# Moving the tiles of a hybrid DeltaNet / gMLP layer to other byte offsets, and folding an identity product into the inverse's residual

## The chip, the core and the metric

The kernel runs on one core of a Trainium2 chip. A core has five engines that run their own instruction streams and meet through semaphores: PE (TensorE, matrix products), DVE (VectorE), ACT (ScalarE), POOL (GpSimd) and SP (SyncE, which here issues every DMA). PE has a second row in the profile, PEld, for the loading of the stationary operand. Operands lie in SBUF, a memory of 128 partitions; a tile takes the same byte range of every partition, and "address" below means the byte within a partition. Products are summed in PSUM. The metric is the device time of one execution in microseconds (us); of several runs the median is given.

## What is computed

One layer of a diffusion backbone over 17 tiles of 128 tokens (one tile of context, sixteen of latent tokens), model width 1024:

```
h = rmsnorm(x, norm_mix) * (1 + sc1) + sh1
o = mixer(h)                      # [gated DeltaNet, both directions | gMLP] -> w_out
x = x + ga1 * o
h = rmsnorm(x, norm_ffn) * (1 + sc2) + sh2
x = x + ga2 * (square(relu(h @ w_ff1)) @ w_ff2)        # 1024 -> 4096 -> 1024
y = rmsnorm(x, norm_final)
```

In the DeltaNet every chunk needs a triangular solve:

```
a_mat = where(strict, (k_beta @ k.T) * decay, 0)
sol = triangular_solve(a_mat + I, rhs, lower=True, unit_diagonal=True)
```

## The kernel before

**Products in two pieces.** Nearly all large products are float32 products made of three float32r products: an operand is split into a rounded part H and the rest L, and `mm3` (L222 to L228) issues, for each stationary pair and moving pair, H·H (L226), H·L (L227) and L·H (L228). Each is one matmul with a stationary operand of 128x128 and a moving operand of up to 512 columns.

**Stages, in the order of the program.** First the modulation, the norms and the projections to q, k, v (blocks of 3 tiles, moving operands of 386, 388 or 258 columns, tiles `kH` and `kL`). Then the scan: 34 units (17 tiles, two directions), each with a prepared inverse and a chain of states, between which "fillers" run (the projections to gate, u, v of the gMLP, its spatial product with `wsT`, the output projection and the second norm). Then the MLP: 32 units of the first product (FF1), each 7 products (a Strassen-like scheme over halves of the model width, of the tokens and of the hidden width), and 7 products of the second (FF2).

**The inverse.** `unit(t, d)` prepares the inverse of A = I + strict part of a chunk, in half precision. `X` and `Y` are the approximate inverse and its transpose, built level by level from blocks of 2 to blocks of 128 (`level`, L1047, to L1104). A last step refines it: with A = `AH` + `AL`, L1110 and L1111 form A·Y in PSUM, L1113 (DVE) makes R = I - A·Y as a half-precision tile, and the next step (L1117 to L1124) sums two things into one PSUM tile: for each of 4 heads the product of `X` and `R` (L1120, 128 columns), then one matmul of the identity with the whole of `Y` (L1121, 512 columns). So the result is Y + Y(I - A·Y). ACT then evicts it, scaled, to `T` (L1124), which the chain of states uses. `quad` (L990) issues the 4 products of the heads with one line.

**Order.** The engines' orders are not written out: the framework's scheduler simulates the program when it is built, and orders each engine's instructions by program order and readiness. In the scan, each step carries a time (`at`, `spread`), and fillers get an ordering edge behind a step of the chain.

**Where the tiles lie.** Pools are laid out from the left end of a partition upward in the order in which they are opened, those with `side="right"` from the right end downward. Tiles are rounded up to 32 bytes. In the program before:

| pool | what it holds | address | modulo 128 |
|---|---|---|---|
| `const` | identity, tables, `wsT` at 8,288 | from 1,152 | `wsT`: 96 |
| `small` | small columns, `pick` (first) | from 10,400 | 32 |
| `wp` | 49 tiles of 2,048 bytes: weights, pieces `wH`, `wL`, `zH`, `zL` | from 12,672 | 0 |
| `p1` | first stage, `kH` and `kL`, 1,568 bytes apart | 146,816 and on | 0, 32, 64, 96 in turn |
| `hp`, `scan`, `fp` | the scan's other tiles, fillers' stationary operands | | 0 |
| `prep` (right) | half-precision `AH`, `AL`, `X`, `Y`, `P`, `R`, and `E`, `KK` | 200,672 to 229,344 | 96 |
| `hopB` | 5 tiles of 16,384 bytes, moving operands of the MLP | 113,024 and on | 0 |
| `hopA` (right, after `prep` is closed) | 2 such tiles | 196,576 and 212,960 | 96 |

The right end of a partition, 229,344, is 96 past a multiple of 128.

**Which product reads which tile.** In FF1 the moving operand of product o is a tile `hop` loaded from memory. The products come in the order 1, 5, 6, 7, 3, 2, 4; those of products 1 and 5 lie in `hopA`, the other five in `hopB` (`hop_tile`, L933, and `hop_next` after it). A matmul of FF1 reads 4 runs of 128 columns, 4,096 bytes apart. In FF2 the moving operands are pieces of `w_ff2`, built by `t_build` (L1639) four to a tile; of the 28 tiles in a row, numbers 0, 1 of each five go to `hopA` and 2, 3, 4 to `hopB`. Product n of 0 to 6 uses tiles 4n to 4n+3, one for each q in a pass of 4 x 12 matmuls over one token pair u. So the passes of products n = 0, 1, 2, 5, 6 (9 + 8 + 8 + 8 + 9 = 42 passes) use two tiles of `hopA`, and those of n = 3 and 4 (18 passes) use one. Tile 0 and 1, for q = 0 and 1 of the first product, are in `hopA`, tiles 2 and 3 in `hopB`.

```
def hop_tile(dt, n):
    side, bufs = ("A", 2) if n else ("B", 5)
...
moved.append(hop_tile(F32R, (len(tcount) - 1) % 5 < 2))
...
products = [(1, list(range(9))), (5, list(range(8))), (6, list(range(8))), (7, list(range(9))),
            (3, list(range(9))), (4, list(range(8))), (2, [8] + list(range(8)))]
```

Of the kernel before, what the change touches and what calls it, by code (L numbers as in the profile page):

```python
# [8 lines left out]
F32 = mybir.dt.float32  # L9
F32R = mybir.dt.float32r  # L10
F16 = mybir.dt.float16
BF16 = mybir.dt.bfloat16
AF = mybir.ActivationFunctionType
ALU = mybir.AluOpType
# [3 lines left out]
P = 128  # L18
# [5 lines left out]
H = 4  # L24
# [39 lines left out]
def hybrid_step(  # L64
# [7 lines left out]
    V, A, G, T = nc.vector, nc.scalar, nc.gpsimd, nc.tensor  # L72
# [15 lines left out]
    cp = ctx.enter_context(tc.tile_pool(name="const", bufs=1))  # L88
# [30 lines left out]
    make_identity(nc, ident)  # L119
    ident16 = cp.tile([P, P], F16, name="ident16")  # L120
    V.tensor_copy(ident16, ident)
    nhalf = cp.tile([P, 72], F32, name="nhalf")
    V.memset(nhalf, -0.5)
    zcol = cp.tile([P, KT], F32, name="zcol")
    V.memset(zcol, 0.0)
# [22 lines left out]
    def bc4(ap):  # L148
        return ap.unsqueeze(1).to_broadcast([P, 4, P])
# [18 lines left out]
    wsT = cp.tile([P, 4, P], F32, name="wsT")  # L168
    scond = cp.tile([P, KT, 2], F32, name="scond")

    smp = ctx.enter_context(tc.tile_pool(name="small", bufs=4, reuse_waits="tile"))
    wp = ctx.enter_context(tc.tile_pool(name="wp", bufs=49, reuse_waits="tile"))
    wst = ctx.enter_context(ExitStack())
# [53 lines left out]
            T.matmul(ps, lh, rl, start=False, stop=False, skip_group_check=more)  # L227
            T.matmul(ps, ll, rh, start=False, stop=last and i == n - 1, skip_group_check=more)  # L228

    pick = smp.tile([P, 2, 2], F32, tag="pick", name="pick", bufs=1)  # L230
    V.memset(pick, 0.0)
    V.memset(pick[:, 0, 0:1], 1.0)
    V.memset(pick[:, 1, 1:2], 1.0)
# [42 lines left out]
    with ExitStack() as ph:  # L276
# [499 lines left out]
        side = []  # L776
        for bi in range(len(BLOCKS)):
# [8 lines left out]
            for n, (gi, h) in enumerate(order):  # L786
                u = us[n] if bi == 0 and n < 3 else feature_tile(blk, bi, gi, h)
# [39 lines left out]
                side = []  # L827
# [117 lines left out]
    with ExitStack() as ph:  # L945
        right = ctx.enter_context(ExitStack())
        pp = right.enter_context(tc.tile_pool(name="prep", bufs=1, side="right", reuse_waits="tile"))
# [6 lines left out]
        def pd():  # L954
            return psd.tile([P, 4, P], F32, tag="d", name="pd", bufs=4)
# [7 lines left out]
        def f16(tag, bufs=1):  # L963
            return pp.tile([P, 4, P], F16, tag=tag, name=tag, bufs=bufs)

        def q32(tag, bufs=1, pool=None):
            return (pool or dl).tile([P, 4, P], F32, tag=tag, name=tag, bufs=bufs)
# [10 lines left out]
        identq = f16("identq")  # L978
        V.tensor_copy(identq, bc4(ident16))
        pms = {s: f16(f"P{s}") for s in (2, 4, 8, 16, 32)}  # L980

        def unit(t, d):

            u = {}
            sg = 1 if d == 0 else -1

            def col(tab, h):
                return tab[:, t, d * 4 + h : d * 4 + h + 1]

            def quad(p, lhs, rhs):  # L990
                for h in range(H):
                    T.matmul(p[:, h, :], lhs[:, h, :], rhs[:, h, :], start=True, stop=True)  # L992
# [20 lines left out]
            @prep.append  # L1013
            def _():
                e = s32("E")
                for h in range(H):
                    A.activation(e[:, h, :], u["gb"][:, h, :], AF.Abs, scale=-1.0, bias=col(gcol, h))
                A.activation(e, e, AF.Exp, scale=-1.0)
                es = s32("Es")
                G.affine_select(out=es, in_=e, pattern=[[0, 4], [-sg, P]], compare_op=ALU.is_gt, fill=0.0,  # L1020
                                base=0, channel_multiplier=sg)
                G.affine_select(out=e, in_=e, pattern=[[0, 4], [sg, P]], compare_op=ALU.is_ge, fill=0.0,
                                base=0, channel_multiplier=-sg)
                u["Es"], u["E"] = es, e
# [81 lines left out]
            @prep.append  # L1106
            def _():
                p = pd()
                for h in range(H):
                    T.matmul(p[:, h, :], u["AH"][:, h, :], u["Y"][:, h, :], start=True, stop=False)  # L1110
                    T.matmul(p[:, h, :], u["AL"][:, h, :], u["Y"][:, h, :], start=False, stop=True)  # L1111
                u["R"] = f16("R", 1)
                V.scalar_tensor_tensor(out=u["R"], in0=p, scalar=-1.0, in1=bc4(ident16), op0=ALU.mult,  # L1113
                                       op1=ALU.add)

            @prep.append
            def _():  # L1117
                p = pd()
                for h in range(H):
                    T.matmul(p[:, h, :], u["X"][:, h, :], u["R"][:, h, :], start=h == 0, stop=False)  # L1120
                T.matmul(p, ident16, u["Y"], start=False, stop=True)  # L1121
                u["T"] = q32("T", BT)
                for h in range(H):
                    A.activation(u["T"][:, h, :], p[:, h, :], AF.Copy, scale=col(hbeta, h))  # L1124
# [707 lines left out]
    for j, t in enumerate(range(8, -1, -1)):  # L1832
        st = h2_steps(t, bank, lambda: w512("junk"), w512)
        p = 10 + 19 * j // 2
# [3 lines left out]
    for p, (o, n, b) in enumerate(seq):  # L1838
        u = units[n]
# [25 lines left out]
    for m, (n, i, u, q) in enumerate(todo):  # L1865
# [12 lines left out]
        h, lo = sops.pop(m)  # L1878
# [70 lines left out]
```

## Time and profile before

| | us |
|---|---|
| runs | 2638.01, 2633.96, 2638.87; median 2638.01 |
| the profiled execution, its own time | 2636.78 |
| its span, first to last instruction | 2634.9 |
| mean granted TensorE clock | 0.996 |

The page gives the busy time of each engine and, for 40 slices of the span, busy shares and the granted clock. "Lines" group instructions by line, engine and tiles. A timeline row has the start, the length and the line of an instruction or of several merged ones (xN). Matmuls are pipelined: a 512-column matmul is shown some 0.39 us long though the next begins after some 0.23 us, so what counts for PE is the distance between the starts of successive rows, called the pitch below. Where a short instruction waits in PE's queue behind a streaming one, its start is that of its entry, and the wait shows in the pitch of the row after.

### The profile page before, as it was taken

Reading aid. Unit: us, or ns where it says so; the run is one execution under the profiler, and the core shown is the slowest. Engines: PE = TensorE matmul, PEld = TensorE weight load, DVE = VectorE, ACT = ScalarE, POOL = GpSimd, SP = SyncE. Lnnn points to the kernel's source line nnn. Section 1 sums busy time; section 2 is a strip of 40 time slices with the busy share of each in tenths; the row PEclk is TensorE's granted clock in tenths of the full one; section 3 lists DMA queues with packets and bytes.
Section 4 is the critical chain, followed back from the end, with each engine's and each line's share of the span. In section 5 each row is a group of like instructions: output and inputs, shape, how many; then the busy total and the mean of one; then the engine's idle time right before and its main releaser. Section 6 shows DMA issues by size and latency. Waiting matters only on the chain.

```text
span 2634.9 us, 44534 instructions
## 1 busy us (share of the span) xinstructions
PE 2592.2 (98%) x15458; PEld 2161.4 (82%) x15458; DVE 1778.8 (68%) x3676; ACT 1236.1 (47%) x3074; POOL 229.8 (9%) x448
## 2 busy tenths in 40 slices
PE   9999999999999999999999999999999999999998
PEld 5999998787887777778888888888887887888887
DVE  5867646765666868885678876666665556674874
ACT  4755555655555757763345543333332432243441
POOL 3211112210111111110000000000000000000000
PEclk9999999999999999999999999999999999999999
DMA  8967638654445657885868788444479979776772
GB/s 289 303 200 224 195 109 266 217 165 147 156 155 176 210 176 268 281 291 172 288 202 253 222 278 296 124 116 115 121 249 364 329 257 311 252 256 210 230 250 96
DMA packets 499751, 580.86 MB, mean 220 GB/s; under 512 B 35692, under 2 KB 298268, under 8 KB 495942
## 3 DMA queue, kind: packets, MB, share of 16 engines
q1 hardware_dynamic: 499526, 578.03, 67.7%
q8 instruction: 121, 1.98, 0.3%
q14 instruction: 104, 0.85, 0.1%
HBM read 398.14 MB, written 179.74 MB: 219 GB/s over the span
## 4 chain that ended last, share of the span: by engine, by line
PE 86%; DMA 5%; DVE 5%; ACT 1%; issue 1%; SPq 1%; POOL 1%; DVEq 0%; POOLq 0%; ACTq 0%
PE f L227 16%; PE f L228 16%; PE f L226 16%; PE pj L226 7%; PE pj L228 6%; PE pj L227 6%; PE pd L992 3%; PE f L1589 2%; PE pm L226 1%; PE pm L227 1%; PE pm L228 1%; PE pt L606 1%; DMA raw<-in_w_mod_dram 1%; PE pd L1165 1%; PE pd L1166 1%
## 5 line engine op out<-in xcount | busy, mean ns | idle before, releaser
L226 PE MATMUL f<-hop,zH 128*128 128x512 f32 x960 | 376.5, 392 | 1.2 <-ACT zH L1475 1.2
L227 PE MATMUL f<-hop,zH 128*128 128x512 f32 x960 | 377.1, 393 | 0.0
L228 PE MATMUL f<-hop,zL 128*128 128x512 f32 x960 | 376.9, 393 | 0.0
L226 PE MATMUL f<-hop,wH 128*128 128x512 f32 x896 | 356.8, 399 | 0.0
L227 PE MATMUL f<-hop,wH 128*128 128x512 f32 x896 | 351.2, 392 | 0.0
L228 PE MATMUL f<-hop,wL 128*128 128x512 f32 x896 | 349.9, 392 | 0.0
L1475 ACT CAST zH<-zraw 128x512 fp32r<-128x512 f32 x240 | 146.6, 620 | 287.9 <-DVE zraw L1469 87.8
L226 PEld LDWEIGHTS f<-hop,zH 128*128 128x128 f32 x960 | 180.4, 188 | 43.8 <-ACT zH L1475 1.6
L1469 DVE TENSOR_TENSOR zL<-zraw,zH 128x512 fp32r<-128x512 f32 x240 | 162.4, 686 | 78.7 <-ACT zH L1475 65.5
L228 PEld LDWEIGHTS f<-hop,zL 128*128 128x128 f32 x960 | 180.3, 188 | 42.0 <-issue 0.9
L227 PEld LDWEIGHTS f<-hop,zH 128*128 128x128 f32 x960 | 180.1, 188 | 41.7 <-issue 0.9
L228 PEld LDWEIGHTS f<-hop,wL 128*128 128x128 f32 x896 | 168.2, 188 | 37.2
L227 PEld LDWEIGHTS f<-hop,wH 128*128 128x128 f32 x896 | 168.5, 188 | 34.6
L226 PEld LDWEIGHTS f<-hop,wH 128*128 128x128 f32 x896 | 168.6, 188 | 34.5
L226 PE MATMUL pj<-kH,wH 128*128 128x386 f32 (+2 forms) x568 | 190.4, 338 | 2.2 <-ACT junk L582 1.1
L228 PE MATMUL pj<-kH,wL 128*128 128x386 f32 (+2 forms) x568 | 189.7, 334 | 0.0
L227 PE MATMUL pj<-kL,wH 128*128 128x386 f32 (+2 forms) x568 | 189.0, 334 | 0.0
L183 POOL TENSOR_TENSOR r<-rsq,nhalf 128x1 f32<-128x1 f32 (+1 forms) x38 | 23.1, 608 | 1445.0 <-DVE rsq L182 1445.0
L552 DVE SCALAR_TENSOR_TENSOR cv<-pj,vec,cv 128x384 f32<-128x384 f32 (+2 forms) x164 | 87.0, 539 | 54.1 <-ACT cv L549 52.8
L226 PEld LDWEIGHTS pj<-kH,wH 128*128 128x128 f32 x568 | 107.0, 189 | 7.9 <-issue 4.7
L1475 ACT CAST wH<-s 128x512 fp32r<-128x512 f32 x96 | 59.4, 621 | 106.3 <-DVE s L1469 106.1
L227 PEld LDWEIGHTS pj<-kL,wH 128*128 128x128 f32 x568 | 107.4, 189 | 0.5
(397 smaller groups left out, 5763.1 us busy)
## 6 DMA issues: line engine op xcount, KB each, us to landing
zraw<-z_d SPq DMA_DIRECT2D x212, 256.0 KB
raw<-in_w_ff_dram SPq DMA_DIRECT2D x128, 256.0 KB
hop<-hop_d SPq DMA_DIRECT2D x28, 1024.0 KB
z_d<-c SPq DMA_DIRECT2D x96, 256.0 KB
zraw<-s_d SPq DMA_DIRECT2D x96, 256.0 KB
raw<-in_w_mod_dram SPq DMA_DIRECT2D x80, 256.0 KB
r<-in_w_ff_dram SPq DMA_DIRECT2D x80, 256.0 KB
s_d<-s SPq DMA_DIRECT2D x64, 256.0 KB
```

Source lines behind the costliest of these rows:

```text
L183: G.tensor_tensor(out=out, in0=t[:np_, :n], in1=nhalf[:np_, :n], op=ALU.pow)
L226: T.matmul(ps, lh, rh, start=first and i == 0, stop=False, skip_group_check=more)
L227: T.matmul(ps, lh, rl, start=False, stop=False, skip_group_check=more)
L228: T.matmul(ps, ll, rh, start=False, stop=last and i == n - 1, skip_group_check=more)
L552: V.scalar_tensor_tensor(out=cv[:, o : o + m], in0=ps[:, s + sh : s + sh + m], scalar=convw[:, w, j : j + 1], in1=cv[:, o : o + m], op0=AL ...
L606: T.matmul(ps[:, i * P : (i + 1) * P], kTt[:, i * P : (i + 1) * P], rhs[:, i * P : (i + 1) * P], start=True, stop=True)
L992: T.matmul(p[:, h, :], lhs[:, h, :], rhs[:, h, :], start=True, stop=True)
L1165: T.matmul(p[:, h, :], u["qT"][:, h, :], s[:, h, :], start=True, stop=False)
L1166: T.matmul(p[:, h, :], u["QK"][:, h, :], u["vn"][:, h, :], start=s is None, stop=True)
L1469: V.tensor_tensor(out=out, in0=a, in1=b, op=op)
L1475: A.copy(h, src)
L1589: T.matmul(ps[:, c : c + P], self.raw[m, kh][:, kp, :], x0[kh][:, kp, :], start=first and kp == 0, stop=last and kp == 3)
```

## The change

Three things are done.

1. `nhalf`, a constant of 72 columns, gets 80: 288 bytes become 320, and all that lies behind it in `const` moves up by 32 bytes, `wsT` to 8,320 = 65 x 128.
2. `pick` leaves the pool `small` (32 bytes there, so that `wp` and all behind it on the left stay at their addresses) for a new pool `edge`, the first one on the right side, of 12 x 2 float32 = 96 bytes. Everything else on the right moves down by 96 bytes: `hopA` comes to 196,480 = 1535 x 128 and 212,864, `prep` to tiles at multiples of 128.
3. A half-precision tile `two16`, twice the identity, is made at the scan's beginning. L1113 then makes R = 2I - A·Y, the step after it computes X and R alone, Y(2I - A·Y), and the matmul of the identity with `Y` is dropped. `two16` takes 256 bytes in `prep`.

```diff
-    nhalf = cp.tile([P, 72], F32, name="nhalf")
+    nhalf = cp.tile([P, 80], F32, name="nhalf")
...
+    edge = ctx.enter_context(tc.tile_pool(name="edge", bufs=1, side="right"))
     smp = ctx.enter_context(tc.tile_pool(name="small", bufs=4, reuse_waits="tile"))
...
-    pick = smp.tile([P, 2, 2], F32, tag="pick", name="pick", bufs=1)
+    pick = edge.tile([P, 12, 2], F32, name="pick")[:, 0:2, :]
...
         pms = {s: f16(f"P{s}") for s in (2, 4, 8, 16, 32)}
+        two16 = pp.tile([P, P], F16, tag="two16", name="two16")
+        V.tensor_scalar_mul(two16, ident16, 2.0)
...
-                V.scalar_tensor_tensor(out=u["R"], in0=p, scalar=-1.0, in1=bc4(ident16), op0=ALU.mult,
+                V.scalar_tensor_tensor(out=u["R"], in0=p, scalar=-1.0, in1=bc4(two16), op0=ALU.mult,
                                        op1=ALU.add)
...
                 p = pd()
-                for h in range(H):
-                    T.matmul(p[:, h, :], u["X"][:, h, :], u["R"][:, h, :], start=h == 0, stop=False)
-                T.matmul(p, ident16, u["Y"], start=False, stop=True)
+                quad(p, u["X"], u["R"])
```

## Prediction

> **What bounds the kernel now.** I read the page's first part, then a table of the stages, the waits of PE, and then PE's timeline at a few places, since the change touches almost nothing but PE's operands.
>
> ```profile
> span 2634.9 us, 44534 instructions
> PE 2592.2 (98%) x15458; PEld 2161.4 (82%) x15458; DVE 1778.8 (68%) x3676; ACT 1236.1 (47%) x3074; POOL 229.8 (9%) x448
> ...
> 457.60:1240.00 782.40, 754.38 (x6443) 616.44 (x6443) 557.38 (x1486) 471.33 (x1343) 111.69 (x139) 0.99 0.61 199
> 1240.00:1955.90 715.90, 715.90 (x3444) 597.38 (x3443) 497.40 (x819) 288.38 (x576) 7.67 (x11) 1.00 0.65 205
> 1955.90:2624.00 668.10, 666.91 (x2881) 539.32 (x2880) 422.86 (x688) 225.99 (x415) 10.24 (x16) 1.00 0.77 262
> ```
>
> The three stretches are the scan, FF1 with its lead-in, and FF2; the columns are length, then busy time and instructions of PE, PEld, DVE, ACT, POOL, granted clock, DMA share, GB/s. From 1240 us on PE is never idle for more than 1.2 us in all, at full clock, with DVE at 69% and 63% and DMA at 65% and 77%: what shortens PE's stream there shortens the kernel by as much. In the scan PE is idle 782.4 - 754.4 = 28.0 us; half of it is one wait, for a product's eviction in the inverse:
>
> ```profile
> PE pd L1074 <- DVE P L1066: 13.8, 19, 2.1
> ```
>
> So there PE's time counts mostly, but a part of a gain may go into that wait. The profiled execution took 2636.8 us; the median of the three runs is 2638.0, so 1.2 us goes on top of every time worked out below.
>
> **Part 1, where the MLP's moving tiles begin.** The busy time of a line hides the question, because the pitch counts. One pass of the first product of FF2 shows it; rows are the first matmuls of q = 0, 1, 2, 3 and of the next pass, 12 matmuls apart:
>
> ```profile
> 2000.27 0.40 PE L226 MATMUL f<-hop,zH 128*128 128x512 f32 x1
> ...
> 2003.09 0.39 PE L226 MATMUL f<-hop,zH 128*128 128x512 f32 x1
> ...
> 2005.89 0.40 PE L226 MATMUL f<-hop,zH 128*128 128x512 f32 x1
> ...
> 2008.65 0.39 PE L226 MATMUL f<-hop,zH 128*128 128x512 f32 x1
> ...
> 2011.37 0.40 PE L226 MATMUL f<-hop,zH 128*128 128x512 f32 x1
> ```
>
> Twelve matmuls take 2.82 us for q = 0 and 2.80 for q = 1, whose tiles are in hopA at 96 modulo 128; 2.76 for q = 2 and 2.72 for q = 3, in hopB at 0. The first group on hopB after hopA is still 0.04 above the second, so the stream needs some matmuls to settle; the first on hopA is likewise dearer than the second. FF1 has the same steps, here product 5 (hopA) and, further on in the unit, product 2 (hopB):
>
> ```profile
> 1642.26 0.39 PE L226 MATMUL f<-hop,wH 128*128 128x512 f32 x1
> ...
> 1645.06 0.40 PE L226 MATMUL f<-hop,wH 128*128 128x512 f32 x1
> ...
> 1655.07 0.39 PE L226 MATMUL f<-hop,wH 128*128 128x512 f32 x1
> ...
> 1657.80 1.05 PE L1589 MATMUL f<-x,raw 128*128 128x128 f32 x8
> ```
>
> These are 2.80 and 2.73 us. If all seven tiles lie at 0, every group should take 2.72 (0.2267 a matmul). A pass or unit with two tiles of hopA then gains 0.10 + 0.08 + 0.04 = 0.22 us, one with a single tile 0.10 + 0.04 = 0.14. FF2 has 42 of the first kind and 18 of the second: 9.2 + 2.5 = 11.7 us. FF1 has 32 units of the first kind (product 1 on hopA and product 6, the first on hopB, taken as q = 0 and q = 2 above): 7.0. Together 18.7 us, with nothing else moved in these stages.
>
> All of hopA lies higher in SBUF than all of hopB, so the two groups alone don't tell offset from place. Two things decide for the offset. The first stage, whose kH and kL tiles lie below hopA at offsets 0, 32, 64 and 96 in turn, never settles; ten pitches of 386 columns from the first to the last row here:
>
> ```profile
> 140.01 0.34 PE L226 MATMUL pj<-kH,wH 128*128 128x386 f32 x1
> ...
> 141.79 0.34 PE L227 MATMUL pj<-kL,wH 128*128 128x386 f32 x1
> ```
>
> That is 0.178 each, where 0.2267 x 386/512 would be 0.171: 4% above, as hopA's 2.80 to 2.82 is 3 to 4% above 2.72. And half-precision products read prep, in the same high place, at 0.0575 us for 128 columns (the R, X rows below: 0.23 for four), no more per column than a group on hopB. The bounds of this part: 0 if it is the place, 18.7 if it is the offset; I take 18.7, as both kinds of row lean that way.
>
> [...]
>
> **Part 2, the identity product.** 34 matmuls of 512 half-precision columns with their weight loads go; four products and the eviction stay.
>
> ```profile
> 766.76 0.22 PE L1111 MATMUL pd<-Y,AL 128*128 128x128 f16 x1
> 766.79 0.47 PE L226 MATMUL pj<-wH,hH 128*128 128x512 f32 x1
> 767.10 0.39 PE L227 MATMUL pj<-wL,hH 128*128 128x512 f32 x1
> ...
> 770.39 0.39 PE L1120 MATMUL pd<-R,X 128*128 128x128 f16 x4
> 770.62 0.38 PE L1121 MATMUL pd<-Y,ident 128*128 128x512 f16 x1
> 770.64 0.58 PE L226 MATMUL pj<-wH,hH 128*128 128x512 f32 x1
> 771.06 0.39 PE L227 MATMUL pj<-wL,hH 128*128 128x512 f32 x1
> 771.29 0.40 PE L228 MATMUL pj<-wH,hL 128*128 128x512 f32 x1
> 771.52 0.72 PE L1249 MATMUL pm<-vg,wsT 128*128 128x128 f32 x5
> ...
> L1121 PE MATMUL pd<-Y,ident x34: 379/379/379, 496.2 to 1239.6; 128*128 128x512 f16 x34
> ```
>
> The four R, X begin 0.0575 apart (0.23 up to the matmul behind them), the last at 770.56; the filler's second matmul begins at 771.06, 0.50 later. In the step before, four pairs of the same half-precision form are followed by a filler at once: from the last at 766.76 to its second matmul is 0.34. The dropped matmul was partly cover for the filler's float32 weight load, which now shows. So 0.16 us a unit, 34 units: 5.4 us. The ends: 0, if PE merely waits longer for the inverse's evictions, and 34 x 0.23 (512 columns, four times the 0.0575 of 128) = 7.8 if what follows needs no cover. I take 5.4: most of the scan's waits are elsewhere, and the units' own order is kept. T's eviction starts earlier by as much. DVE's R reads another tile of the same form. The new tile costs DVE one operation on a quarter of the columns of the first row here, among DVE's work before the first unit, in a stretch where PE still has fillers:
>
> ```profile
> 443.33 0.29 DVE L979 COPY identq<-ident 128x512 f16<-128x512 f16 x1
> 443.66 1.10 DVE L1065 COPY P<-identq 128x512 f16<-128x512 f16 x5
> 450.49 0.69 DVE L1080 TENSOR_TENSOR QK<-QK,E 128x512 f32<-128x512 f32 x1 [5.73 <-POOL E L1022]
> ```
>
> At most 0.29 us, once, and nothing if DVE's pause of 5.7 us behind the copies to P covers it; if that cover is gone, the first unit's chain is 0.3 late. I take 0. Widening a memset by 8 columns and moving pick cost nothing that a row shows.
>
> **Part 3, the scan's operands.** wsT and the half-precision tiles come to 0. Their own products, at 0.0575 for 128 columns, run at the pace of hopB's groups already, and I count nothing on them. What may gain is the fillers between them: 771.06 to 771.29 to 771.52 is 0.23 each, 0.003 above 0.2267, as a stream that has been unsettled. Some 1,800 such matmuls (fillers of the gMLP and output projections) give 5 us at most, nothing at least. [...] I take 1.0.
>
> **Sum.** 18.7 + 5.4 + 1.0 = 25.1 us less: 2636.8 - 25.1 = 2611.7 for a profiled execution, 2612.9 beside the median.
>
> **Rivals.**
>
> *The place, not the offset.* hopA is slow because it lies at the top of a partition. For it: every slow group lies there, every fast one below. Against: the first stage's pitches. Then only 5.4 goes: 2638.0 - 5.4 = 2632.6. It is also what a change would do that doesn't do what its title says.
>
> *The scan keeps its time.* The inverse is a chain through DVE and ACT, and L1074's wait of 13.8 us grows by what PE saves; the scheduler also orders the scan anew, since its simulated times change. Then 18.7 goes: 2619.3. For it: the 28 us of idle PE; against: PE is busy 96% of the scan, so waits are the exception.
>
> *Slower, by the clock.* PE's granted clock halves after idle stretches in the scan:
>
> ```profile
> 457.60:462.60 5.00, 2.18 (x9) 1.00 1.05 397
> 462.60:472.90 10.30, 5.65 (x33) 0.50 1.05 389
> ...
> 616.20:619.60 3.40, 3.40 (x20) 0.50 0.69 227
> ```
>
> Here the columns are length, PE busy, clock, DMA. Such a window of 3.4 us costs 1.7 us of a busy PE. If the shorter PE work per unit (0.16 of some 23 us) leaves a longer idle stretch at each inverse, and each of 34 units gets a window more, that is 58 us: 2613 + 58 = 2671. It decides from 15 windows on (25.1 / 1.7). The trace has few such stretches against 19 waits on L1074 alone, so it is far off. [...]
>
> **How the numbers follow.** Forecast 0.63, scan keeps its time 0.17, place 0.12, clock 0.08. The forecast's own spread: 18.7 give or take 1 (rounded rows), part 2 up to 7.8, part 3 0 to 5, and the scan's new order, which I let move 4 us either way, a seventh of its idle time. Lowest 2638.0 - 18.7 - 7.8 - 5 - 2 = 2604.5. Upward the range takes in the scan rival with the order's 4 and 2 more: 2625. What is left out, place and clock, is 0.20. A difference of 0.2% (5.3 us) is what a measurement can tell. Forecast and scan rival are faster by more; of the place rival, 5.4 against 5.3, half. Faster 0.86, same 0.06, slower 0.08.
>
> **What would show it.** Groups of 12 at 2.72 us in every pass of FF2 and unit of FF1 (a pass of 10.88), FF2 shorter by some 11.7 and FF1 by 7.0: part 1. No L1121, 0.34 us from the last R, X to the filler's second matmul, and a scan shorter by 5 to 6: part 2. Fillers at 0.227 in long runs: part 3. Wrong would be: passes that still take 11.1, a scan no shorter, or more windows at half clock.

## The result and the profile after

| | before | after |
|---|---|---|
| median of four runs, us | 2638.44 | 2615.35 |
| lowest to highest, us | 2633.96 to 2641.21 | 2612.01 to 2620.43 |
| the profiled execution, its own time, us | 2636.78 | 2614.33 |
| its span, us | 2634.9 | 2612.6 |

The ratio is 0.991, 95% interval 0.9896 to 0.9924, which is 20 to 27 us of 2638; the medians differ by 23.1 us. The forecast was 2612.9. The page's first lines of the kernel after, and its stretches (length, busy time and instructions of PE, PEld, DVE, ACT, POOL, granted clock, DMA share, GB/s), cut at the first matmul of the scan, at 1240 us and at the first matmuls of FF1 and FF2:

```profile
span 2612.6 us, 44469 instructions
PE 2572.1 (98%) x15424; PEld 2157.7 (83%) x15424; DVE 1778.0 (68%) x3677; ACT 1237.3 (47%) x3074; POOL 229.9 (9%) x448
```

```profile
459.80:1240.00 780.20, 756.85 (x6434) 617.71 (x6435) 556.68 (x1494) 471.94 (x1349) 113.21 (x140) 0.99 0.61 201
1240.00:1268.10 28.10, 28.10 (x149) 23.95 (x148) 19.29 (x37) 8.12 (x20) 1.01 (x1) 1.00 0.52 185
1268.10:1944.60 676.50, 676.33 (x3274) 568.82 (x3273) 475.20 (x772) 278.75 (x549) 5.71 (x9) 1.00 0.66 206
1944.60:2603.30 658.70, 657.51 (x2888) 540.64 (x2887) 424.85 (x688) 226.97 (x415) 11.31 (x16) 1.00 0.78 266
```

PE has 34 matmuls less (15458 to 15424) and is as full as before. These are FF1 and FF2 of the kernel before, cut in the same way:

```profile
1273.40:1955.90 682.50, 682.50 (x3273) 569.03 (x3272) 475.11 (x772) 278.76 (x549) 5.65 (x9) 1.00 0.65 204
1955.90:2625.80 669.90, 668.71 (x2889) 540.78 (x2887) 422.86 (x688) 225.99 (x415) 10.24 (x16) 1.00 0.77 261
```

The counts agree to one matmul at the edges of the cuts; the time does not. All parts of both profiles, in us:

| | before | after | difference |
|---|---|---|---|
| scan, from its first matmul to FF1 | 814.8 | 808.3 | -6.5 |
| FF1, first matmul to FF2 | 682.5 | 676.5 | -6.0 |
| FF2, first to last matmul | 669.9 | 658.7 | -11.2 |
| ahead of the scan | 458.6 | 459.8 | +1.2 |
| behind FF2 | 9.1 | 9.3 | +0.2 |
| span | 2634.9 | 2612.6 | -22.3 |

PE's timeline of the kernel after, one pass of FF2's first product; each row is 12 matmuls behind the one above (L227 is the L226 of before):

```profile
1944.59 0.39 PE L227 MATMUL f<-hop,zH 128*128 128x512 f32 x1
...
1947.31 0.39 PE L227 MATMUL f<-hop,zH 128*128 128x512 f32 x1
...
1950.03 0.39 PE L227 MATMUL f<-hop,zH 128*128 128x512 f32 x1
...
1952.74 0.39 PE L227 MATMUL f<-hop,zH 128*128 128x512 f32 x1
...
1955.46 0.39 PE L227 MATMUL f<-hop,zH 128*128 128x512 f32 x1
```

Every group takes 2.72 us, a pass 10.87, where before it was 2.82, 2.80, 2.76 and 2.72. FF1 shows the same in products 5 and 6 of the unit that the prediction read. There product 5 took 2.80, and product 6, from 1645.06 to the single products (L1589) in the first row here, 2.76; the other rows are those of the kernel after:

```profile
1647.82 1.05 PE L1589 MATMUL f<-x,raw 128*128 128x128 f32 x8
...
1633.60 0.39 PE L227 MATMUL f<-hop,wH 128*128 128x512 f32 x1
...
1636.32 0.39 PE L227 MATMUL f<-hop,wH 128*128 128x512 f32 x1
...
1639.04 1.05 PE L1590 MATMUL f<-x,raw 128*128 128x128 f32 x8
```

Both are 2.72. In the scan, the products of R and X are now issued by `quad` (L995), and a filler follows at once. The first row is from before, the load of that filler's weights, beside the dropped matmul; the others are from after:

```profile
770.62 0.19 PEld L226 LDWEIGHTS pj<-wH,hH 128*128 128x128 f32 x1
...
768.89 0.39 PE L995 MATMUL pd<-R,X 128*128 128x128 f16 x4
769.06 0.19 PEld L227 LDWEIGHTS pj<-wH,hH 128*128 128x128 f32 x1
769.09 0.48 PE L227 MATMUL pj<-wH,hH 128*128 128x512 f32 x1
769.40 0.39 PE L228 MATMUL pj<-wL,hH 128*128 128x512 f32 x1
```

The four R, X begin 0.0575 apart, the last thus at 769.06; the filler's second matmul begins 0.34 behind it, where before it was 0.50. The load of 0.19 us ran while the dropped matmul streamed; now it begins behind the last R, X. PE's longest waits in the scan, and the two stretches of the scan at half clock:

```profile
PE pd L1077 <- DVE P L1069: 9.8, 16, 1.9
PE pd L1065 <- ACT Y L1080: 5.7, 10, 1.5
```

```profile
462.40:479.50 17.10, 12.28 (x62) 8.02 (x63) 14.48 (x37) 12.44 (x33) 7.12 (x7) 0.50 0.84 309
...
936.80:940.20 3.40, 3.40 (x14) 2.36 (x12) 0.90 (x3) 1.47 (x5) 0.00 (x0) 0.50 0.89 283
```

The wait for P was 13.8 and is 9.8. The stretch of half clock at the scan's beginning is 17.1 long instead of 10.3; the one at 616 us is gone.

### The profile page after: what moved, and what is told of

The parts are those of the page before. It is cut to its first block, busy times and chain, and to the rows that moved or that the text cites. A ratio compares the mean times of both kernels' runs of the same rounds, so it can differ in the third digit from the quotient of the medians.

```text
span 2612.6 us, 44469 instructions
## 1 busy us (share of the span) xinstructions
PE 2572.1 (98%) x15424; PEld 2157.7 (83%) x15424; DVE 1778.0 (68%) x3677; ACT 1237.3 (47%) x3074; POOL 229.9 (9%) x448
## 4 chain that ended last, share of the span: by engine, by line
PE 86%; DMA 6%; DVE 4%; ACT 1%; issue 1%; POOL 0%; SPq 0%; DVEq 0%; POOLq 0%; ACTq 0%
PE f L227 16%; PE f L229 16%; PE f L228 16%; PE pj L227 6%; PE pj L229 6%; PE pj L228 6%; PE pd L995 3%; PE f L1590 2%; PE pm L227 2%; PE pm L229 1%; PE pm L228 1%; DMA raw<-in_w_mod_dram 1%; PE pt L607 1%; PE pd L1166 1%; PE pd L1167 1%
## 5 line engine op out<-in xcount | busy, mean ns | idle before, releaser
L227 PE MATMUL f<-hop,zH 128*128 128x512 f32 x960 | 373.4, 389 | 1.2 <-ACT zH L1476 1.2
L227 PE MATMUL f<-hop,wH 128*128 128x512 f32 x896 | 355.3, 397 | 0.2 <-issue 0.2
L227 PEld LDWEIGHTS f<-hop,zH 128*128 128x128 f32 x960 | 180.2, 188 | 39.8 <-ACT zH L1476 1.6
L227 PEld LDWEIGHTS f<-hop,wH 128*128 128x128 f32 x896 | 168.5, 188 | 33.1 <-issue 0.9
L227 PE MATMUL pj<-kH,wH 128*128 128x386 f32 (+2 forms) x568 | 190.4, 338 | 1.7 <-ACT junk L583 1.1
L227 PEld LDWEIGHTS pj<-kH,wH 128*128 128x128 f32 x568 | 107.0, 189 | 7.3 <-issue 4.7
```

The source lines that it names most:

```text
L227: T.matmul(ps, lh, rh, start=first and i == 0, stop=False, skip_group_check=more)
```

## The experiments

### The two halves of the change by themselves

First the offsets alone: `two16` and the dropped product are undone.

```diff
-        two16 = pp.tile([P, P], F16, tag="two16", name="two16")
...
-                V.scalar_tensor_tensor(out=u["R"], in0=p, scalar=-1.0, in1=bc4(two16), op0=ALU.mult,
+                V.scalar_tensor_tensor(out=u["R"], in0=p, scalar=-1.0, in1=bc4(ident16), op0=ALU.mult,
...
+                T.matmul(p, ident16, u["Y"], start=False, stop=True)
```

> The kernel before with the offsets moved (nhalf, edge, pick) and the identity product left in. If the pitch of the MLP's matmuls follows the offset of the moving tile alone: every group of 12 takes 2.72 us in FF1 and FF2, FF2 11 us and FF1 6 us shorter than before, as in the changed kernel, and the whole 17 us shorter than before (ratio 0.9935), with the scan within 3 us of before. If the scan's tiles gain by their offsets too, the scan is shorter by 1 to 5 us more. If the changed kernel's gain came from somewhere else, the groups would differ.

Then the residual alone: `nhalf` and `pick` are as before.

```diff
-    nhalf = cp.tile([P, 80], F32, name="nhalf")
+    nhalf = cp.tile([P, 72], F32, name="nhalf")
...
-    edge = ctx.enter_context(tc.tile_pool(name="edge", bufs=1, side="right"))
...
-    pick = edge.tile([P, 12, 2], F32, name="pick")[:, 0:2, :]
+    pick = smp.tile([P, 2, 2], F32, tag="pick", name="pick", bufs=1)
```

> The kernel before with two16 and without the identity product, offsets as before. If the dropped matmul is worth what the rows around it say: 0.34 us from the last R, X to the second filler matmul instead of 0.50, the scan 5.4 us shorter (ratio 0.998), the MLP as before with its groups of 2.82, 2.80, 2.76, 2.72. If the inverse's chain takes the gain back as waiting: the scan is no shorter, and the waits of PE in the scan are longer by about 5 us than the 28 us of before.

| | time, us | ratio to before | FF1 | FF2 | scan |
|---|---|---|---|---|---|
| offsets only | 2621.62 | 0.9931 [0.9919, 0.9944] | 676.8 | 658.7 | 814.4 |
| residual only | 2635.16 | 0.9983 [0.9974, 0.9992] | 682.5 | 669.9 | 812.2 |

The parts add up: 0.9931 x 0.9983 = 0.9914, and the whole change has 0.991. The offsets bring 18.2 us (14.8 to 21.4; 0.0069 x 2639.8, the median of before beside these runs), all of it in FF1 and FF2: the scan of that kernel is 0.4 us from that of before. The residual alone brings 4.5 us (2.1 to 6.9) and leaves FF1 and FF2 as they were, to a tenth of a us.

The scan's time has two parts that the program doesn't fix: PE's idle time, and what half clock costs. These are the rows for its length up to 1240 us and the stretches at half clock, first of before (the two other stretches are in the prediction), then of the offsets alone, then of the residual alone, whose four stretches of 20.40 us are summed in the last row:

```profile
458.60:1240.00 781.40, 754.27 (x6442) 616.43 (x6443) 556.90 (x1485) 470.33 (x1342) 111.69 (x139) 0.99 0.61 199
...
940.50:943.90 3.40, 3.25 (x24) 2.97 (x25) 1.68 (x4) 1.80 (x5) 0.47 (x1) 0.50 0.86 224
```

```profile
459.70:1240.00 780.30, 751.84 (x6437) 614.43 (x6436) 555.23 (x1482) 468.98 (x1338) 111.08 (x139) 0.99 0.61 199
...
465.10:478.80 13.70, 9.10 (x57) 6.41 (x57) 11.83 (x32) 11.43 (x31) 4.30 (x6) 0.50 0.83 303
```

```profile
459.20:1240.00 780.80, 753.95 (x6417) 615.50 (x6418) 554.67 (x1488) 471.48 (x1349) 112.43 (x139) 0.99 0.61 200
...
sum 20.40, PE 15.95 PEld 11.33 DVE 14.15 ACT 11.05 POOL 4.28; mean PE 3.99 PEld 2.83 DVE 3.54 ACT 2.76 POOL 1.07
```

Idle is length less PE's busy time (first row); the cost of half clock is taken as half of PE's busy time in it, an estimate. What is left of the scan is PE's work at full clock:

| us | scan | idle | cost of half clock | left |
|---|---|---|---|---|
| before | 814.8 | 27.1 | 6.2 | 781.5 |
| offsets only | 814.4 | 28.5 | 4.6 | 781.4 |
| residual only | 812.2 | 26.9 | 8.0 | 777.4 |
| after | 808.3 | 23.3 | 7.8 | 777.1 |

The residual takes 4.1 to 4.4 us of work off PE; the offsets take nothing (0.1) off the scan. In the profiled execution of after PE also idled 3.8 us less, and half clock cost it 1.7 more. Neither part alone shows that shorter idle time. The eight kernels further below, all without the identity product, have 776.5 to 778.3 us left by the same reckoning, so the gain in work is there at whatever addresses the tiles have.

### Offset or place: hopB at 96, hopA at 0

A tile of 96 bytes ahead of the five `hopB` tiles turns the layout of before around.

```diff
     hops["B"] = ctx.enter_context(tc.tile_pool(name="hopB", bufs=1, reuse_waits="tile"))
+    shift = hops["B"].tile([P, 24], F32, tag="shift", name="shift", bufs=1)
```

> The changed kernel with 96 bytes of padding ahead of hopB, so that hopB's five tiles lie at 96 modulo 128 and hopA's two at 0: the mirror image. If the offset decides: groups on hopB take 2.80 (2.82 the first after hopA), the first on hopA after hopB 2.76; in the first product's passes q = 0 takes 2.76, q = 1 2.72, q = 2 2.82, q = 3 2.80; FF2 and FF1 together some 35 us longer than in the changed kernel (FF1: 5 products of 7, some 0.4 us a unit; FF2: some 0.25 to 0.35 a pass). If hopA was slow for its place at the top of SBUF, groups on hopB stay at 2.72.

It took 2648.1 us in its one run, where the median of before beside it was 2639.8. PE's timeline of the first pass of FF2:

```profile
1964.41 0.39 PE L227 MATMUL f<-hop,zH 128*128 128x512 f32 x1
...
1967.16 0.39 PE L227 MATMUL f<-hop,zH 128*128 128x512 f32 x1
...
1969.88 0.40 PE L227 MATMUL f<-hop,zH 128*128 128x512 f32 x1
...
1972.70 0.39 PE L227 MATMUL f<-hop,zH 128*128 128x512 f32 x1
...
1975.50 0.40 PE L227 MATMUL f<-hop,zH 128*128 128x512 f32 x1
```

2.75 and 2.72 for the two tiles of `hopA`, 2.82 and 2.80 for those of `hopB`: the mirror image of before. The place falls; the slow groups follow the address. FF1 and FF2 take 689.1 and 672.8 us, together 26.7 more than after; the expectation of 35 was too high.

### How much of an offset: hopA at 64 and at 32

`pick` is made smaller, and `hopA` comes to 64 or 32 modulo 128.

```diff
-    pick = edge.tile([P, 12, 2], F32, name="pick")[:, 0:2, :]
+    pick = edge.tile([P, 4, 2], F32, name="pick")[:, 0:2, :]
```

> The changed kernel with an edge pool of 32 bytes, so that hopA (and prep in the scan) lie at 64 modulo 128. If what counts is a line of 128 bytes: groups on hopA cost 2.76 to 2.82 us again, FF1 and FF2 together 10 to 17 us longer than in the changed kernel. If it is a line of 64 bytes or less: 2.72 everywhere, as in the changed kernel.

The other has `[P, 8, 2]`:

> The changed kernel with an edge pool of 64 bytes: hopA and prep at 32 modulo 128. If a line of 128 or of 64 bytes counts: slow groups on hopA, 2.76 to 2.82 us; if a line of 32 or 16 bytes: 2.72 everywhere. If each offset has its own price, 32, 64 and 96 give three different groups.

Heads of the groups in the first pass of FF2, at 64 and then at 32:

```profile
1944.91 0.40 PE L227 MATMUL f<-hop,zH 128*128 128x512 f32 x1
...
1947.67 0.39 PE L227 MATMUL f<-hop,zH 128*128 128x512 f32 x1
...
1950.42 0.40 PE L227 MATMUL f<-hop,zH 128*128 128x512 f32 x1
```

```profile
1954.09 0.40 PE L227 MATMUL f<-hop,zH 128*128 128x512 f32 x1
...
1956.89 0.39 PE L227 MATMUL f<-hop,zH 128*128 128x512 f32 x1
...
1959.69 0.40 PE L227 MATMUL f<-hop,zH 128*128 128x512 f32 x1
```

At 64 a settled group takes 2.75 us, a third of the excess; at 32 it takes 2.80, as at 96. FF2 takes 665.2 and 669.1 us, between the 658.7 of after and the 669.9 of before. At 64, FF1 and FF2 together are 9.4 us longer than after, just under the 10 to 17 of one case expected and far from the nothing of the other: the offsets tried have three prices, not two. The kernels took 2621.1 and 2634.2 us, where the kernel before took 2645.1 on that chip, with one run of each.

### The stationary operand

All this moved the moving tiles. Here `wp`, which holds the stationary pieces `wH`, `wL`, `zH`, `zL`, goes to 96, and every moving tile stays at 0 (a tile of 32 bytes ahead of `hopB` makes up for it there).

```diff
-    nhalf = cp.tile([P, 80], F32, name="nhalf")
+    nhalf = cp.tile([P, 72], F32, name="nhalf")
...
+    shift = hops["B"].tile([P, 8], F32, tag="shift", name="shift", bufs=1)
```

> The changed kernel with nhalf at 72 columns again, which moves everything on the left by 32 bytes to 96 modulo 128, and 32 bytes of padding ahead of hopB, which holds hopB at 0. In the MLP the moving tiles lie at 0 and the stationary ones (wp) at 96: if the moving operand alone counts, groups stay at 2.72; if the stationary one counts too, they rise to between 2.73 and 2.82. In the scan the fillers' moving and stationary tiles are at 96: if their short runs never settle anyway, the scan is within 3 us of the changed kernel's; if offset counts there, 1,800 fillers at some 0.006 more make it some 10 us longer.

Then `wp`, `hopA` and `hopB` all at 96:

```diff
-    nhalf = cp.tile([P, 80], F32, name="nhalf")
+    nhalf = cp.tile([P, 72], F32, name="nhalf")
...
-    pick = edge.tile([P, 12, 2], F32, name="pick")[:, 0:2, :]
+    pick = edge.tile([P, 16, 2], F32, name="pick")[:, 0:2, :]
```

> The changed kernel with nhalf at 72 columns and an edge pool of 128 bytes: the stationary tiles (wp) and all moving tiles of the MLP at 96 modulo 128. If only the distance between the two operands counts (both 96, distance 0): groups of 2.72 us everywhere, FF1 and FF2 as in the changed kernel (676 and 659 us). If each operand must lie on a line by itself: 2.80 or more, FF1 and FF2 at least as long as with the stationary tiles alone at 96 (692 and 678 us).

And three different offsets: `wp` at 96, `hopA` at 32, `hopB` at 64.

```diff
-    nhalf = cp.tile([P, 80], F32, name="nhalf")
+    nhalf = cp.tile([P, 72], F32, name="nhalf")
...
-    pick = edge.tile([P, 12, 2], F32, name="pick")[:, 0:2, :]
+    pick = edge.tile([P, 8, 2], F32, name="pick")[:, 0:2, :]
...
+    shift = hops["B"].tile([P, 24], F32, tag="shift", name="shift", bufs=1)
```

> Stationary tiles at 96, hopA at 32, hopB at 64 modulo 128. If the distance counts: hopA (distance 64) settles at the 2.747 us that moving 64 against stationary 0 gave, hopB (distance 32) at 2.80. If each operand counts by itself: hopA (32) and hopB (64) both at 2.80 or more, since the stationary tile at 96 alone gave 2.80.

First rows of two passes of FF2, 48 matmuls apart, with the stationary operand at 96, then with all at 96; then the groups of one pass with three offsets:

```profile
1967.55 0.40 PE L227 MATMUL f<-hop,zH 128*128 128x512 f32 x1
...
1978.75 0.40 PE L227 MATMUL f<-hop,zH 128*128 128x512 f32 x1
```

```profile
1948.96 0.39 PE L227 MATMUL f<-hop,zH 128*128 128x512 f32 x1
...
1959.84 0.39 PE L227 MATMUL f<-hop,zH 128*128 128x512 f32 x1
```

```profile
1962.58 0.40 PE L227 MATMUL f<-hop,zH 128*128 128x512 f32 x1
...
1965.34 0.39 PE L227 MATMUL f<-hop,zH 128*128 128x512 f32 x1
...
1968.08 0.40 PE L227 MATMUL f<-hop,zH 128*128 128x512 f32 x1
...
1970.89 0.39 PE L227 MATMUL f<-hop,zH 128*128 128x512 f32 x1
...
1973.69 0.39 PE L227 MATMUL f<-hop,zH 128*128 128x512 f32 x1
```

A pass takes 11.20 us (four times 2.80) with the stationary tiles at 96 and all moving ones at 0; it takes 10.88 with both at 96. So neither offset counts by itself: what counts is the distance of the two. Both kernels move everything on the left by the same 32 bytes, so it is no other tile there that makes the difference. With three offsets the groups on `hopA` (distance 64) take 2.76 and 2.74, those on `hopB` (distance 32) 2.81 and 2.80. Put together:

| distance of moving and stationary tile, bytes (modulo 128) | settled group of 12, us | one matmul, ns | seen in |
|---|---|---|---|
| 0 | 2.72 | 226.7 | before (`hopB`), after, all at 96 |
| 64 | 2.75 | 229 | `hopA` at 64; three offsets (`hopA`) |
| 32 or 96 | 2.80 | 233 | before (`hopA`), `hopB` at 96, `hopA` at 32, stationary at 96, three offsets (`hopB`) |

In all of these kernels the starts of the two operands of a matmul of the MLP differ by these 0 to 96 bytes and a multiple of 512. So the runs don't say whether a distance of 128 or 256 is as good as one of 0; that the rule repeats every 128 bytes is not shown.

The times, of one run each, go with the table: 2656.2 us with the stationary operand at 96 (FF1 692.2, FF2 677.8), where the kernel before took 2645.1 on that chip; 2618.7 with both at 96 (675.9, 658.7) and 2646.3 with three offsets, where it took 2637.9. From 658.7, 60 passes of four groups 0.08 dearer give 60 x 4 x 0.08 = 19.2 us; the stationary operand at 96 adds 19.1. Its scan, expected within 3 us of after or some 10 longer, took 815.1 us, 6.8 longer; PE's work at full clock in it is 777.4, as in after, and the rest is idle time and half clock.

### The first stage

The prediction read the unsettled pitch of the first stage (386 columns, 0.178 instead of 0.171 us) as a sign of the offsets of `kH` and `kL`. Here all of these tiles begin at multiples of 128 (and the small tile `mrow` leaves their pool).

```diff
-                kH = p1.tile([P, 388], F32R, tag="h", name="kH", bufs=24)
-                kL = p1.tile([P, 388], F32R, tag="h", name="kL", bufs=24)
+                kH = p1.tile([P, 416], F32R, tag="h", name="kH", bufs=24)
+                kL = p1.tile([P, 416], F32R, tag="h", name="kL", bufs=24)
```

> The changed kernel with kH and kL of the first stage in tiles of 416 columns (1,664 bytes, 13 x 128), so that each begins at a multiple of 128, and the small row of the modulation in another pool to make room; 386 columns are still read of each. If the start of a moving tile decides: the pitch of the first stage settles at 0.171 to 0.172 us instead of 0.178, and the stage is up to 1,700 x 0.006 = 10 us shorter (ratio to before 0.988). If the length of a read counts too (386 columns end 8 bytes into a line of 128): the pitch stays at 0.175 to 0.178 and the time is that of the changed kernel (0.991).

Ten pitches, from the first to the last row:

```profile
137.70 0.33 PE L227 MATMUL pj<-kH,wH 128*128 128x386 f32 x1
...
139.46 0.34 PE L228 MATMUL pj<-kL,wH 128*128 128x386 f32 x1
```

They are 0.176 each. It took 2616.6 us, ratio 0.9912 [0.9899, 0.9926], which can't be told from the 0.991 of the change. Over the stage, the mean of 1,134 such pitches is 0.1814 us, where it is 0.1826 in before and in after. So the tile's offset modulo 128 is not what keeps the first stage unsettled. (The tiles still lie 13 x 128 bytes apart, at 0, 128, 256 and 384 modulo 512.) The other candidate is the length that is read. In FF2, products 5 and 6 now read 480 of the 512 columns and products 7 and 3 read 482, except the first and the last matmul of a sum, so the last columns of these sums lack most of their terms:

```diff
+        cut = {5: 480, 6: 480, 7: 482, 3: 482}.get(i, 512)
...
+                c = 512 if b or s else cut
+                T.matmul(ps[:, :c], st[:, kp, :], t[:, r].rearrange("p k d -> p (k d)")[:, :c], start=b, stop=s)
```

> The changed kernel, in which the second product's matmuls read fewer columns, beside the first and last of each sum: 480 (15 x 32) in products 5 and 6, 482 in products 7 and 3; the columns left out are missing from the result. All tiles lie at 0. If the length of a read counts as its start does (lines of 32 float32): 480 columns settle at 480/512 of 0.2267 = 0.2125 us, 482 do not settle and take 0.218 to 0.222, 3 to 4% more, as the first stage with 386 columns does. If only the start counts: 482 columns settle at 0.2134.

18 pitches of 480 columns, then 27 of 482:

```profile
2134.97 0.59 PE L1885 MATMUL f<-hop,zH 128*128 128x480 f32 x2
2135.41 0.37 PE L1885 MATMUL f<-hop,zL 128*128 128x480 f32 x1
2135.62 0.59 PE L1885 MATMUL f<-hop,zH 128*128 128x480 f32 x2
2136.05 0.38 PE L1885 MATMUL f<-hop,zL 128*128 128x480 f32 x1
2136.27 0.59 PE L1885 MATMUL f<-hop,zH 128*128 128x480 f32 x2
...
2138.87 0.59 PE L1885 MATMUL f<-hop,zH 128*128 128x480 f32 x2
...
2330.02 0.60 PE L1885 MATMUL f<-hop,zH 128*128 128x482 f32 x2
...
2335.96 0.38 PE L1885 MATMUL f<-hop,zH 128*128 128x482 f32 x1
```

480 columns take 3.90 / 18 = 0.2167, 482 take 5.94 / 27 = 0.2200. In proportion to 512 they would take 0.2125 and 0.2134. A length of 482 thus costs 3% at distance 0, as much as the first stage's 386 columns lose; but 480, a length of 15 x 128 bytes, does not settle either: its pitches alternate (0.21 from 2135.41, 0.22 from 2136.05). The length plays a part; by which rule stays open.

## Why the prediction was right, and where it wasn't

**Part 1, 18.7 us.** The step stands: groups of 12 go to 2.72 in FF2, and the offsets alone bring 18.2 us (14.8 to 21.4). By stages it was 17.2 of 18.7. FF2's 11.7 measured 11.2: the differences of rows rounded to 0.01 us gave 0.22 and 0.14 a pass. FF1's 7.0 measured 6.0, or 0.19 a unit instead of 0.22, the term of this part that was most off: the unit was priced with 0.10 for product 1, as for FF2's first group. In 12 of the 16 units of FF1's second half product 1 gained 0.08 (2.90 to 2.82), product 5 0.08 and product 6 0.04. The other four run as two pairs, whose four groups on `hopA` stand together, and gained 0.33 a pair.

**The reason behind part 1.** The conclusion was right, its two arguments were not. The first stage's pitch, which decided there for the offset, does not follow the offset of its tiles (0.176 with all at 0). The half-precision products at 0.0575 were read as speaking against the place; but `prep` lay at 96 modulo 128, so they spoke against the offset just as much. They fit the distance: `X` and `R` both lie in `prep`, at distance 0 before and after. That the offset won was thus partly luck; the mirror image of `hopB` at 96 is what shows it. And "where the moving tiles begin" was half of it: the stationary tiles in `wp` happened to lie at 0, so the distance looked like an offset.

**Part 2, 5.4 us.** The step from the last R, X to the filler's second matmul went from 0.50 to 0.34, just the 0.16 that was taken, in all 29 units where a filler follows in both kernels (29 x 0.16 = 4.6); the rest are two units where another half-precision product of the inverse follows (0.30 to 0.08, nearly all of the 0.23; the load there, a half-precision one, takes 0.10 and not 0.19) and three where the scheduler moved a filler. PE's work at full clock in the scan fell by 4.1 to 4.4, the time of the residual alone by 4.5 (2.1 to 6.9). The estimate was some 1 us high.

**Part 3, 1.0 us.** No run shows this term: the scan keeps 781.4 of 781.5 us of work with the offsets alone. The mean pitch of successive fillers of 512 columns is 0.2305 us before and 0.2304 after. Their operands lay at distance 0 already. Within a run of fillers the pitches 2 to 4 have medians of 0.231 to 0.235 us and those from the eighth on 0.227 (before), and two thirds of the runs are 3 or 6 matmuls long: most end before they settle. The one distance in the scan's fillers that the change did move, that of `wsT` to its moving operand, left their pitch at 0.112.

**The sum.** The profile fell by 22.3 where 25.1 were counted. The scan's share, 6.5 for 6.4, agrees by chance: 4.4 of work, 3.8 less idle time and 1.7 more of half clock. What made PE idle less is not settled: the seven kernels with the same program and other addresses have scans of 808.2 (`hopA` at 64) to 817.0 us (`hopB` at 96), with 25.0 to 28.8 us of idle time and 6.4 to 12.4 of half clock. The 23.3 us of idle time in after lie below all of them.

**The rivals.** That the place counts fell with the mirror image. That the scan keeps its time fell with the residual alone, whose interval lies below 1. The clock: half clock covers 20.5 us of the scan against 17.1 before, where 15 stretches more were needed to lose the gain.

## What to carry to other kernels

Where float32r products stream back to back with a stationary operand each, compare the starting addresses of the two operands before anything is restructured: a pool that begins 32 or 96 bytes off a multiple of 512 from the other cost 3% of the pitch here, 64 bytes 1%, and a padding of some tens of bytes brought it back. Look at the pitch of twelve like matmuls, not at their busy time (the rows here show 0.39 to 0.40 us at each of the three pitches), and at a group well behind a change of tiles. The dropped matmul was worth what it had delayed the next one: 0.16 us of the 0.23 that its columns took where the filler's float32 weight load of 0.19 us had run beside it, 0.22 where a half-precision load of 0.10 us had.

## What the hardware showed beyond that

The pitch depended on the two operands together: moving only the stationary tiles from 0 to 96 raised a group of twelve from 2.72 to 2.80 us, and with the moving tiles at 96 too it took 2.72. Why the distance counts, no run shows.

After a change of distance the stream took about a group of twelve to settle: in the kernel before, the first group behind the slow tiles takes 2.76 us, the next 2.72. And at distance 0 a read of 480 columns, which is 15 x 128 bytes, still alternated between 0.21 and 0.22 us, while one of 512 columns held 0.2267.
